# Last group of a PEER layer: gate and residual folded in earlier, last v tiles loaded earlier, final norm in a written order

## The chip, the cores and the metric

The kernel runs on one core of a Trainium2 chip. The metric is the device time of one execution in microseconds (us); 3119.42 is the median of three runs. Engines: PE multiplies matrices into PSUM banks, DVE, ACT and POOL work on SBUF and PSUM tiles, SP issues the loads and stores, POOL also issues the indexed loads (gathers). Each engine works through its own list in order and stops at a step whose data or buffer isn't there yet.

## The reference

```python
# 1024 tokens, width 1024; first sub-layer (projection, convolution + RWKV-7 scan, norm) gives x
h2 = adaln(x, shift2, scale2)
# 8 heads pick 16 of 16384 experts each: experts, gates
u_sel = jnp.take(peer_u, eb, axis=0)
z = jnp.einsum('td,tkd->tk', hb, u_sel)
act = jax.nn.gelu(z, approximate=False) * gb
y2 = jnp.einsum('tk,tkd->td', act, jnp.take(peer_v, eb, axis=0))
x = layer_norm(ALPHA * x + gate2 * y2, ln2_g, ln2_b)
```

## The kernel before

The first 1300 us (the front part) compute the first sub-layer, the routing and `x1`, the input of the last residual. Then the expert layer runs in two ways side by side.

Five of the eight token tiles of 128 rows (NT = 5, `DT` gives their numbers) are computed densely: 32 groups of four blocks of 128 experts. In a group, each block e has an up part (192 products for all four, in eight PSUM banks `mg` one after another, three banks in all), then ACT applies gelu (L1420), DVE multiplies with the routing weights `gmat` (L1422), ACT and DVE split the result into `ah` and `al` (L1423, L1424). Then comes the down part, `down(t, half, p)`: for each tile and half of the width 12 products of `ah`, `al` with the group's v tiles, and DVE adds the bank to `y_acc` (L1452). The weights come on SP as `uraw` and `vraw` through three common buffers; ACT and POOL split them (`split_w`, L1314, L1316). A group reads four v tiles, c = 0 to 3; c = 0, 1 serve the first half of the width, 2, 3 the second.

The other three tiles (`GT`) are gathered: `gather(t)` fetches one u row or v row per token and selected expert, 256 gathers of 512 KB a tile, issued by POOL (L1273) into `grow` buffers (GBUF = 7, and one `gland` buffer once space is free), each used up by one DVE step (L1279 for u, L1286 for v, summed in `gy`, a PSUM tile). `gather_to` advances these by the share of the groups that is done, so that all are called for by group 30; `residual_norm` ends a tile. A scheduler, which knows what each step needs, sets the order of the steps on each engine; the code sets priorities.

In group 31 the v tiles are multiplied by the gate on DVE (`vraw`, L1312) before they are split, so that the last products come out gated. `finish` loads v tiles 2 and 3, loads `x1` of the five tiles into `xres`, gates `y_acc` (L1358, three tiles on DVE, two on POOL), adds ALPHA times `x1` (L1363 on DVE, L1360 and L1361 on ACT and POOL), then adds each bank (L1372, with the row sum; L1375 and bn_stats for the last tile), gets the variance from squares on ACT (L1383), scales on ACT (L1391), multiplies with the norm's gain (L1392) and adds its offset (L1393) on DVE and stores the halves (L1394).

Of the kernel before, what the change touches and what calls it, by code (L numbers as in the profile page):

```python
# [60 lines left out]
FT = 5  # L61
FV = 3
# [33 lines left out]
def layer_kernel(ctx, tc, x, cols, c_row, cond_w, w_in, w2a2, g2, w_out, ln_rows, wq, keys, peer_u, peer_ut, peer_v, peer_vt, out):  # L96
# [136 lines left out]
    def rsqrt(mv):  # L233

        rs = small.tile([128, 1], F32, name="rstd")
        nr = small.tile([128, 1], F32, name="rnew")
# [2 lines left out]
        V.tensor_mul(nr, rs, rs)
# [1000 lines left out]
    more, turn = [], [0]  # L1240

    def landing():
# [5 lines left out]
        if more and turn[0] % (GBUF + 1) == 0:  # L1248
# [3 lines left out]
    def gather(t):  # L1252
# [17 lines left out]
        for i in range(256):  # L1270
            while k < 256 and len(pend) < GBUF - 1 + len(more):
# [74 lines left out]

    def finish(down, vs):
        vs += [load_v(31, 2), load_v(31, 3)]
        xts = []
        for t in range(NT):  # L1350
            xts.append(de.tile([128, D], F32, tag="raw" if t < 2 else "uhi" if t < 4 else "ulo", name="xres",
                               bufs=3 if t < 2 else 2))
            ld(xts[t], x1_d[DT[t]])
        row_pair([(1, ln_rows[3])])
        gather_to(1)
        for t in range(NT):
            E = V if t < FV else G
            E.tensor_mul(y_acc[:, t], y_acc[:, t], lnr[2])  # L1358
            if t >= FV:
                A.activation(xts[t], xts[t], AF.Copy, scale=ALPHA)  # L1360
                G.tensor_add(xts[t], xts[t], y_acc[:, t])  # L1361
            else:
                V.scalar_tensor_tensor(xts[t], xts[t], ALPHA, y_acc[:, t], op0=OP.mult, op1=OP.add)  # L1363
        for t in range(NT):
            xt = xts[t]
            st = small.tile([128, 2, 6], F32, name="bnst")
            sums = small.tile([128, 4], F32, name="fsum")
            for half, hs in enumerate(halves):
                p = md() if half else mg()
                down(t, half, p)  # L1370
                if t < NT - 1:
                    V.scalar_tensor_tensor(xt[:, hs], p, 1.0, xt[:, hs], op0=OP.mult, op1=OP.add,  # L1372
                                           accum_out=sums[:, half:half + 1])
                else:
                    V.tensor_add(xt[:, hs], p, xt[:, hs])  # L1375
                    V.bn_stats(st[:, half, :], xt[:, hs])
            b = small.tile([128, 1], F32, name="nbias")
            if t < NT - 1:
                mv = small.tile([128, 2], F32, name="bnmv")
                V.tensor_scalar(mv[:, 0:1], sums[:, 0:1], sums[:, 1:2], -1.0 / D, op0=OP.add, op1=OP.mult)  # L1380
                sq = grow()
                for half, hs in enumerate(halves):
                    A.activation(sq[:, hs], xt[:, hs], AF.Square, bias=mv[:, 0:1], accum_out=sums[:, 2 + half:3 + half])  # L1383
                V.tensor_scalar(mv[:, 1:2], sums[:, 2:3], sums[:, 3:4], 1.0 / D, op0=OP.add, op1=OP.mult)
                m, r = rsqrt(mv)
                V.tensor_mul(b, m, r)
            else:
                m, r = moments(st)
                V.scalar_tensor_tensor(b, m, -1.0, r, op0=OP.mult, op1=OP.mult)
            for hs in halves:  # L1390
                A.activation(xt[:, hs], xt[:, hs], AF.Identity, bias=b, scale=r)  # L1391
                V.tensor_mul(xt[:, hs], xt[:, hs], lnr[0][:, hs])  # L1392
                (V if t >= NT - 1 - FT else G).tensor_add(xt[:, hs], xt[:, hs], lnr[1][:, hs])  # L1393
                ld(out[128 * DT[t]:128 * DT[t] + 128, hs], xt[:, hs])  # L1394
# [3 lines left out]
    for g in range(32):  # L1398
        gm = g_next
        if g < 31:  # L1400
            g_next = load_g(g + 1)
# [109 lines left out]
```

## Time and profile before

| what | value |
|---|---|
| timed runs | 3113.9, 3119.42, 3121.65 us |
| profiled execution | 3138.46 us, of which the span is 3136.6 |
| busy: PE, DVE, POOL, ACT | 2958.2, 2386.3, 1808.7, 1187.2 us |
| last product on PE | starts at 3116.09 us |
| last store, on SP | issued at 3133.2 us |

Times in the rows are us from the start of the span: a row of the engines in order of time has start, duration, engine, line, operation, output and inputs with shapes, and in brackets how long the engine stood before it and what ended that. Line numbers (L1286) are those of the kernel before. For the kernel after, lines move: the gathers' steps are L1300 and L1307, the gmat step L1530, `al` L1532, the sums L1560, the gate on v L1333, `fold` L1355 to L1357, and all steps written through `InOrder` carry L1382.

### The profile page before, as it was taken

The page shows a single profiled execution, that of the slowest core. Times are in us where ns is not written, and L with a number is a line of the kernel's source. Part 1 is how long each engine was busy: PE and PEld are TensorE (multiplying, and loading weights), DVE is VectorE, ACT ScalarE, POOL GpSimd, SP SyncE. Part 2 cuts the span into 40 slices and gives each one's busy share as a digit, 9 for nine tenths or more (in the row PEclk, how much of TensorE's full clock was granted, in tenths as well). Part 3 has the DMA queues.
Part 4 walks back from the last instruction along what each step waited for, and adds up shares of the span by engine and source line. Part 5 has one row for each costly group of instructions (what it writes and reads, how often), then busy time and mean ns, then how long its engine had stood idle before and what let it go on. Part 6 is the DMA issues. An engine that isn't in the chain of part 4 may idle for free.

```text
span 3136.6 us, 54848 instructions
## 1 busy us (share of the span) xinstructions
PE 2958.2 (94%) x20416; PEld 2616.1 (83%) x20416; DVE 2386.3 (76%) x5392; ACT 1187.2 (38%) x2238; POOL 1808.7 (58%) x1419
## 2 busy tenths in 40 slices
PE   6979998989899789999999999999999999999997
PEld 4748667878778688898898899989999898999986
DVE  6276654446876989369999999997778787777878
ACT  5562443333345657842332233322223132222324
POOL 2434112223352443477777786877778688787774
PEclk9989998968888999999999999999999999999999
DMA  8878857768666797899999999999999999999995
GB/s 318 307 206 310 263 153 217 259 217 298 216 220 241 281 330 287 330 339 346 321 331 336 313 338 322 346 356 340 337 336 339 335 337 348 331 340 347 329 353 190
DMA packets 431851, 945.77 MB, mean 302 GB/s; under 512 B 92464, under 2 KB 234208, under 8 KB 411104
## 3 DMA queue, kind: packets, MB, share of 16 engines
q1 hardware_dynamic: 318112, 497.62, 47.0%
q0 software_dynamic: 110592, 402.70, 34.4%
q10 hardware_dynamic: 2880, 41.94, 3.3%
q8 instruction: 160, 2.62, 0.3%
q14 instruction: 107, 0.88, 0.1%
HBM read 800.76 MB, written 141.39 MB: 300 GB/s over the span
## 4 chain that ended last, share of the span: by engine, by line
PE 61%; DVE 18%; DMA 5%; ACT 3%; issue 3%; POOL 1%; SPq 1%; DVEq 0%; ACTq 0%; POOLq 0%
PE mg L1418 23%; PE md L1434 21%; PE mm L216 5%; PE mm L870 2%; DVE grow L1279 2%; PE mgate L1108 1%; PE mm L528 1%; DMA cw<-cond_w 1%; DVE gy L1286 1%; DVE mask L1094 1%; DVE yacc L1452 1%; PE bank L733 1%; PE bank L707 1%; PE bank L675 1%; ACT oa L1100 1%
## 5 line engine op out<-in xcount | busy, mean ns | idle before, releaser
L1418 PE MATMUL mg<-h2h,uhi 128*128 128x320 f32 x2024 | 626.8, 310 | 8.2 <-DVE al L1424 8.2
L1418 PE MATMUL mg<-h2h,ulo 128*128 128x320 f32 x2024 | 626.0, 309 | 0.1
L1418 PE MATMUL mg<-h2l,uhi 128*128 128x320 f32 x2024 | 625.5, 309 | 0.0
L1434 PE MATMUL md<-vhi,al 128*128 128x512 f32 x1260 | 490.6, 390 | 0.0
L1434 PE MATMUL md<-vlo,ah 128*128 128x512 f32 x1260 | 489.1, 390 | 0.0
L1434 PE MATMUL md<-vhi,ah 128*128 128x512 f32 x1260 | 484.9, 390 | 0.2 <-issue 0.2
L1286 DVE SCALAR_TENSOR_TENSOR gy<-grow,gz,gy 128x1024 f32<-128x1024 f32 x349 | 446.2, 1279 | 6.5 <-DMA grow<-peer_v,eid 5.5
L1279 DVE SCALAR_TENSOR_TENSOR grow<-grow,gh 128x1024 f32<-128x1024 f32 x363 | 435.5, 1209 | 16.0 <-DMA grow<-peer_u,eid 15.8
L1273 POOL DMA_INDIRECT grow<-peer_u,eid x363 | 342.6, 944 | 171.1 <-DVE grow L1279 57.3
L1273 POOL DMA_INDIRECT grow<-peer_v,eid x352 | 332.9, 946 | 164.8 <-DVE gy L1286 69.5
L1418 PEld LDWEIGHTS mg<-h2h,uhi 128*128 128x128 f32 x2024 | 380.5, 188 | 16.2 <-DVE al L1424 11.0
L1418 PEld LDWEIGHTS mg<-h2l,uhi 128*128 128x128 f32 x2024 | 380.5, 188 | 5.9
L1418 PEld LDWEIGHTS mg<-h2h,ulo 128*128 128x128 f32 x2024 | 380.4, 188 | 3.8 <-POOL ulo L1316 0.6
L1316 POOL TENSOR_TENSOR vlo<-vraw,vhi 128x1024 fp32r<-128x1024 f32 x128 | 309.1, 2416 | 35.3 <-ACT vhi L1314 31.8
L1316 POOL TENSOR_TENSOR ulo<-uraw,uhi 128x1024 fp32r<-128x1024 f32 x128 | 309.3, 2416 | 19.3 <-ACT uhi L1314 17.0
L1452 DVE TENSOR_TENSOR yacc<-md,yacc 128x512 f32<-128x512 f32 x300 | 204.8, 685 | 136.0 <-PE md L1434 94.7
L1434 PEld LDWEIGHTS md<-vlo,ah 128*128 128x128 f32 x1260 | 236.5, 188 | 47.4
L1101 POOL TENSOR_TENSOR ob<-mask,selt 128x384 f32<-128x384 bf16 x160 | 140.2, 890 | 234.2 <-DVE mask L1094 99.4
L1434 PEld LDWEIGHTS md<-vhi,ah 128*128 128x128 f32 x1260 | 236.1, 188 | 45.1 <-issue 0.6
L1434 PEld LDWEIGHTS md<-vhi,al 128*128 128x128 f32 x1260 | 236.5, 188 | 44.1
L1314 ACT ACTIVATE vhi<-vraw 128x1024 fp32r<-128x1024 f32 x128 | 134.9, 1054 | 335.8 <-DMA vraw<-peer_vt 311.2
L216 PE MATMUL mm<-hhi,wsplit 128*128 128x512 f32 x672 | 228.0, 413 | 8.5 <-ACT gsig L399 5.4
(430 smaller groups left out, 5778.9 us busy)
## 6 DMA issues: line engine op xcount, KB each, us to landing
uraw<-peer_ut SPq DMA_DIRECT2D x128, 512.0 KB
vraw<-peer_vt SPq DMA_DIRECT2D x128, 512.0 KB
wsplit<-split_wq SPq DMA_DIRECT2D x48, 1024.0 KB
G_d<-stage ACTq DMA_DIRECT2D x20, 2048.0 KB
gmat<-G_d SPq DMA_DIRECT2D x32, 1024.0 KB
cw<-cond_w SPq DMA_DIRECT2D x48, 512.0 KB
wsplit<-split_w_out SPq DMA_DIRECT2D x24, 1024.0 KB
split_w_in<-wsplit SPq DMA_DIRECT2D x22, 1024.0 KB
```

The costliest lines, as they stand in the source:

```text
L216: T.matmul(pt, l[:, k, :], r[k], start=i == 0, stop=i == 3 * KD - 1)
L528: T.matmul(pt[:, 128 * g:128 * g + 128], dg[:, 128 * j:128 * j + 128], ubuf[ct][:, g, LAGS - 1 - m:LAGS - 1 - m + 128], start=m == 0, stop ...
L870: T.matmul(acc[t], l[k][:, ts], r, start=k == 0 and q == 0, stop=k == KD - 1 and q == 2)
L1101: G.tensor_mul(ob[:, :3], mb[:, :3], gt[:, c:c + 3, None].to_broadcast([128, 3, 128]))
L1273: G.indirect_dma_start(out=r, out_offset=None, in_=peer_u if k < 128 else peer_v, in_offset=bass.IndirectOffsetOnAxis(ap=eid[:, k % 128:k ...
L1279: V.scalar_tensor_tensor(r, r, 1.0, ht, op0=OP.mult, op1=OP.mult, accum_out=z[:, i:i + 1])
L1286: V.scalar_tensor_tensor(y, r, z[:, i - 128:i - 127], y, op0=OP.mult, op1=OP.add)
L1314: A.activation(hi, raw, AF.Copy)
L1316: G.tensor_sub(lo, raw, hi.bitcast(F32))
L1418: T.matmul(p, l[:, k, :], r[k][:, bs], start=i == 0, stop=i == 3 * KD - 1)
L1434: T.matmul(p, l[:, ts], r[:, e % 2, :], start=e == 0 and q == 0, stop=e == 3 and q == 2)
L1452: ins = V.tensor_add(ya, p, ya)
```

## The change

1. `fold(t)` is called in the second half of group 29's down part, for each tile behind its last sum of that group: it loads `x1` of the tile into the one `gland` buffer, multiplies `y_acc` of the tile by the gate row and adds ALPHA times `x1`, both on DVE. Groups 30 and 31 now both get gated v tiles (before, 31 alone). The gate row is loaded in group 28 into a buffer of its own. The `gland` buffer is given up by the gathers for the last 70 (XLAST).
2. In group 31 all four v tiles are loaded with the four u blocks.
3. Gathers are called for by group 29 in place of 30, but the last 8 steps (HELD), seven gathers and the third tile's norm, are left to `finish`, which places them between the sums.
4. `finish` is written as one order for DVE, ACT and POOL (`InOrder` chains each step behind the one before on its engine; the gathered tile's norm is not chained). Tiles 0 to 2: ACT scales, POOL multiplies with the gain and adds the offset. Tile 3: DVE subtracts the mean and multiplies with the gain (read from PSUM), ACT scales, POOL adds. Tile 4: DVE does both.
5. `residual_norm` takes row sums from the residual step and squares from ACT in place of bn_stats; `rsqrt` has two fused steps in place of three.

```diff
-FT = 5
-FV = 3
+FOLD = 30
+XLAST = 70
+HELD = 8
...
-        V.tensor_mul(nr, rs, rs)
         V.tensor_scalar(mv[:, 1:2], mv[:, 1:2], LN_EPS, -0.5, op0=OP.add, op1=OP.mult)
-        V.tensor_scalar(nr, nr, mv[:, 1:2], 1.5, op0=OP.mult, op1=OP.add)
-        V.tensor_mul(rs, rs, nr)
+        V.scalar_tensor_tensor(nr, rs, mv[:, 1:2], rs, op0=OP.mult, op1=OP.mult)
+        V.scalar_tensor_tensor(rs, nr, 1.5, rs, op0=OP.add, op1=OP.mult)
...
+    def squares(xt, sums):
+        mv = sums[:, 4:6]
+        V.tensor_scalar(mv[:, 0:1], sums[:, 0:1], sums[:, 1:2], -1.0 / D, op0=OP.add, op1=OP.mult)
+        sq = grow()
+        for i, hs in enumerate(halves):
+            A.activation(sq[:, hs], xt[:, hs], AF.Square, bias=mv[:, 0:1], accum_out=sums[:, 2 + i:3 + i])
+        V.tensor_scalar(mv[:, 1:2], sums[:, 2:3], sums[:, 3:4], 1.0 / D, op0=OP.add, op1=OP.mult)
+        return mv
...
     def residual_norm(t, acc):
...
-        parts = [xt[:, 0:512], xt[:, 512:1024]]
-        normalize(parts, parts)
+        mv = squares(xt, sums)
         r = bcast_row(ln_rows[2])
-        V.tensor_mul(xt, xt, r)
+        V.scalar_tensor_tensor(xt, xt, mv[:, 0:1], r, op0=OP.add, op1=OP.mult)
+        m, rs = rsqrt(mv)
         r = bcast_row(ln_rows[3])
+        A.activation(xt, xt, AF.Copy, scale=rs)
         G.tensor_add(xt, xt, r)
...
+    def spare():
+        return bool(more) and done[0] < n_side - XLAST
...
-        if more and turn[0] % (GBUF + 1) == 0:
+        if spare() and turn[0] % (GBUF + 1) == 0:
             return more[0].tile([128, D], F32, name="gland")
...
-        while side and done[0] < frac * n_side:
+        while side and done[0] < min(frac * n_side, n_side - HELD):
...
-        if g == 31 and c % 2 == 0:
+        gated = g >= FOLD
+        if gated and c % 2 == 0:
...
+    def fold(t):
+        xt = more[0].tile([128, D], F32, name="gland")
+        ld(xt, x1_d[DT[t]])
+        V.tensor_mul(y_acc[:, t], y_acc[:, t], lnr[2])
+        V.scalar_tensor_tensor(y_acc[:, t], xt, ALPHA, y_acc[:, t], op0=OP.mult, op1=OP.add)
...
+        def add(t, half):
...
+            down(t, half, p)
+            if t < end:
+                v.scalar_tensor_tensor(yt, p, 1.0, yt, op0=OP.mult, op1=OP.add, accum_out=sums[t][:, half:half + 1])
             else:
+                v.tensor_add(yt, p, yt)
+                v.bn_stats(st[t][:, half, :], yt)
...
+        def root(t):
+            n = small.tile([128, 1], F32, name="rnew")
+            v.reciprocal(rs[t], rs[t])
+            v.tensor_scalar(mv[t][:, 1:2], mv[t][:, 1:2], LN_EPS, -0.5, op0=OP.add, op1=OP.mult)
+            v.scalar_tensor_tensor(n, rs[t], mv[t][:, 1:2], rs[t], op0=OP.mult, op1=OP.mult)
+            v.scalar_tensor_tensor(rs[t], n, 1.5, rs[t], op0=OP.add, op1=OP.mult)
+
+        def scale(t):
+            b = small.tile([128, 1], F32, name="nbias")
+            v.tensor_mul(b, mv[t][:, 0:1], rs[t])
+            for hs in halves:
+                yt = y_acc[:, t, hs]
+                a.activation(yt, yt, AF.Identity, bias=b, scale=rs[t])
+                gq.tensor_mul(yt, yt, lnr[0][:, hs])
+                gq.tensor_add(yt, yt, lnr[1][:, hs])
+                ld(out[128 * DT[t]:128 * DT[t] + 128, hs], yt)
+
+        def centre(t):
+            for hs in halves:
+                v.scalar_tensor_tensor(zt[t][:, hs], y_acc[:, t, hs], mv[t][:, 0:1], gain[0][:, hs],
+                                       op0=OP.subtract if t == end else OP.add, op1=OP.mult)
+
+        def offset(t):
+            for hs in halves:
+                z = zt[t][:, hs]
+                if t == end:
+                    v.scalar_tensor_tensor(z, z, rs[t], lnr[1][:, hs], op0=OP.mult, op1=OP.add)
                 else:
+                    a.activation(z, z, AF.Copy, scale=rs[t])
+                    gq.tensor_add(z, z, lnr[1][:, hs])
+                ld(out[128 * DT[t]:128 * DT[t] + 128, hs], z)
+
+        add(0, 0); gathers(2); add(0, 1); mean(0); gathers(2); add(1, 0); var(0); gathers(2)
+        add(1, 1); root(0); scale(0); mean(1); gathers(1); add(2, 0); var(1); gathers(1)
+        add(2, 1); root(1); scale(1); mean(2); gathers(1)
+        gain[0] = psy.tile([128, D], F32, tag="ghy", name="gain")
+        a.activation(gain[0], lnr[0], AF.Copy)
+        add(3, 0); var(2); add(3, 1); root(2); scale(2); mean(3); add(4, 0); centre(3); var(3)
+        add(4, 1); mean(4); root(3); offset(3); centre(4); root(4); offset(4)
...
-            row_pair([(2, mod_d[5].rearrange("a b -> (a b)")), (0, ln_rows[2])])
+            row_pair([(0, ln_rows[2]), (1, ln_rows[3])])
...
-            if e > 1:
-                vs.append(load_v(g, e - 2))
+            if e > 1 or g == 31:
+                vs.append(load_v(g, e if g == 31 else e - 2))
...
-            gather_to((g + e / 8) / 30)
+            gather_to((g + e / 8) / 29)
...
+                if g == FOLD - 1 and half:
+                    fold(t)
```

(The calls of `finish` stand one to a line in the code.) What the scheduler makes of it at three places, each engine's own list:

DVE in the up part of group 30, before. `gy` steps use up a gather, `mg` and `al` steps belong to the up products:

```order
L1422 TENSOR_TENSOR mg_30359<-mg_30359,gmat_29723 128x320
L1286 SCALAR_TENSOR_TENSOR gy_27826<-grow_29555,gz_25265,gy_27826 128x1024
L1424 TENSOR_TENSOR al_30329<-mg_30359,ah_30328 128x320
L1286 SCALAR_TENSOR_TENSOR gy_27826<-grow_29578,gz_25265,gy_27826 128x1024
L1422 TENSOR_TENSOR mg_30402<-mg_30402,gmat_29723 128x320
L1286 SCALAR_TENSOR_TENSOR gy_27826<-grow_29595,gz_25265,gy_27826 128x1024
```

DVE at that place after the change, from the fold of the third tile to that of the fourth (`gland` holds `x1`):

```order
L1357 SCALAR_TENSOR_TENSOR yacc_14208<-gland_30162,yacc_14208 128x1024
L1307 SCALAR_TENSOR_TENSOR gy_27436<-grow_29079,gz_24947,gy_27436 128x1024
L1530 TENSOR_TENSOR mg_30309<-mg_30309,gmat_29750 128x320
L1333 TENSOR_TENSOR vraw_30419<-vraw_30419,md_30344 128x1024
L1307 SCALAR_TENSOR_TENSOR gy_27436<-grow_29082,gz_24947,gy_27436 128x1024
L1530 TENSOR_TENSOR mg_30355<-mg_30355,gmat_29750 128x320
L1532 TENSOR_TENSOR al_30279<-mg_30309,ah_30278 128x320
L1307 SCALAR_TENSOR_TENSOR gy_27436<-grow_29085,gz_24947,gy_27436 128x1024
L1532 TENSOR_TENSOR al_30354<-mg_30355,ah_30353 128x320
L1307 SCALAR_TENSOR_TENSOR gy_27436<-grow_29108,gz_24947,gy_27436 128x1024
L1357 SCALAR_TENSOR_TENSOR yacc_14208<-gland_30180,yacc_14208 128x1024
```

The residual steps and the gate on v have moved in between the up part's steps, where there were gathers and up steps alone.

SP over the same group, before (the last digits of `x_d_` and `G_d_` number the tensor):

```order
L1310 DMA uraw<-peer_ut 128x1024 x2
L1310 DMA vraw<-peer_vt 128x1024
L1310 DMA uraw<-peer_ut 128x1024
L1310 DMA vraw<-peer_vt 128x1024 x3
L1310 DMA uraw<-peer_ut 128x1024
```

SP there after the change (`x_d_106` to `x_d_109` are `x1` of the second to the fifth tile):

```order
L1331 DMA uraw<-peer_ut 128x1024 x2
L1331 DMA vraw<-peer_vt 128x1024
L1355 DMA gland<-x_d_106 128x1024
L1331 DMA uraw<-peer_ut 128x1024
L1355 DMA gland<-x_d_107 128x1024
L1331 DMA vraw<-peer_vt 128x1024
L1355 DMA gland<-x_d_108 128x1024
L1331 DMA vraw<-peer_vt 128x1024 x2
L1355 DMA gland<-x_d_109 128x1024
L1331 DMA uraw<-peer_ut 128x1024
```

The loads of `x1` now stand between the weights' loads; before, they came in group 31, with one weight tile left behind the first of them.

ACT at the end, before, from the scaling of the gathered tile on (`grow` is the gathered tile in the first row, a scratch tile in the others):

```order
L250 ACTIVATE grow<-grow,nbias,rstd 128x512 x2
L1383 ACTIVATE grow,fsum<-xres,bnmv 128x512 x6
L237 ACTIVATE rstd<-bnmv,eps_ln 128x1 x3
L1383 ACTIVATE grow,fsum<-xres,bnmv 128x512 x2
L1391 ACTIVATE xres<-xres,nbias,rstd 128x512 x6
```

ACT at the end after the change, from the gathered tile's squares on (`rstd` steps are square roots, `gain` the copy to PSUM):

```order
L1233 ACTIVATE grow,bnst<-grow,bnst 128x512 x2
L238 ACTIVATE rstd<-bnst,eps_ln 128x1
L1253 ACTIVATE grow<-grow,rstd 128x1024
L1382 ACTIVATE yacc<-yacc,nbias,rstd 128x512 x2
L1382 ACTIVATE grow,bnst<-yacc,bnst 128x512 x2
L1382 ACTIVATE gain<-gmat 128x1024
L1382 ACTIVATE rstd<-bnst,eps_ln 128x1
```

Squares of one tile and scalings of the tile before it now alternate, with the gathered tile's steps and the copy of the gain among them; before, all squares came first.

More of the change, by code (lines that the diff above doesn't have):

```diff
@@ L1270, in gather @@
         for i in range(256):
[L1271 removed]
+            while k < 256 and len(pend) < GBUF - 1 + spare():
                 r = landing()
@@ L1345, in load_g @@
         return t
[L1347 to L1361, printed above, removed]
-            else:
[L1363 to L1373, printed above, removed]
-                else:
[L1375 to L1394, printed above, removed]
@@ new lines, in layer_kernel, with __init__, __getattr__, issue @@
+    class InOrder:
+        def __init__(self, engine):
+            self.engine, self.last = engine, None
+        def __getattr__(self, name):
+            def issue(*a, **k):
+                with tc.issue_after(self.last.ins) if self.last else nullcontext():
+                    self.last = getattr(self.engine, name)(*a, **k)
+                return self.last
+            return issue
+    def finish(down):
+        v, a, gq = InOrder(V), InOrder(A), InOrder(G)
+        sq = grow()
+        end = NT - 1
+        st, sums, mv, rs = {}, {}, {}, {}
+        zt = {t: de.tile([128, D], F32, tag="raw", name="zres", bufs=3) for t in (end - 1, end)}
+        gain = {}
+        def gathers(n):
+            with tc.issue_after(v.last.ins):
+                for _ in range(n):
+                    step(side)
+        def add(t, half):
+            hs, yt = halves[half], y_acc[:, t, halves[half]]
+            if half == 0:
+                st[t] = small.tile([128, 2, 6], F32, name="bnst")
+                sums[t] = st[t].rearrange("p a b -> p (a b)")
+                mv[t] = sums[t][:, 4:6] if t < end else small.tile([128, 2], F32, name="bnmv")
+            p = md() if half else mg()
+            down(t, half, p)
+            if t < end:
+                v.scalar_tensor_tensor(yt, p, 1.0, yt, op0=OP.mult, op1=OP.add, accum_out=sums[t][:, half:half + 1])
+            else:
+                v.tensor_add(yt, p, yt)
+                v.bn_stats(st[t][:, half, :], yt)
+        def mean(t):
+            rs[t] = small.tile([128, 1], F32, name="rstd")
+            if t == end:
+                v.bn_aggr(mv[t], st[t])
+                a.activation(rs[t], mv[t][:, 1:2], AF.Sqrt, bias=eps_ln)
+                return
+            v.tensor_scalar(mv[t][:, 0:1], sums[t][:, 0:1], sums[t][:, 1:2], -1.0 / D, op0=OP.add, op1=OP.mult)
+            for i, hs in enumerate(halves):
+                a.activation(sq[:, hs], y_acc[:, t, hs], AF.Square, bias=mv[t][:, 0:1],
+                             accum_out=sums[t][:, 2 + i:3 + i])
+        def var(t):
+            v.tensor_scalar(mv[t][:, 1:2], sums[t][:, 2:3], sums[t][:, 3:4], 1.0 / D, op0=OP.add, op1=OP.mult)
+            a.activation(rs[t], mv[t][:, 1:2], AF.Sqrt, bias=eps_ln)
+        def root(t):
[20 more added lines that the diff above has]
+                z = zt[t][:, hs]
+                if t == end:
+                    v.scalar_tensor_tensor(z, z, rs[t], lnr[1][:, hs], op0=OP.mult, op1=OP.add)
+                else:
+                    a.activation(z, z, AF.Copy, scale=rs[t])
+                    gq.tensor_add(z, z, lnr[1][:, hs])
+                ld(out[128 * DT[t]:128 * DT[t] + 128, hs], z)
+        add(0, 0)
+        gathers(2)
+        add(0, 1)
+        mean(0)
+        gathers(2)
+        add(1, 0)
+        var(0)
+        gathers(2)
+        add(1, 1)
+        root(0)
+        scale(0)
+        mean(1)
+        gathers(1)
+        add(2, 0)
+        var(1)
+        gathers(1)
+        add(2, 1)
+        root(1)
+        scale(1)
+        mean(2)
+        gathers(1)
+        gain[0] = psy.tile([128, D], F32, tag="ghy", name="gain")
+        a.activation(gain[0], lnr[0], AF.Copy)
+        add(3, 0)
+        var(2)
+        add(3, 1)
+        root(2)
+        scale(2)
+        mean(3)
+        add(4, 0)
+        centre(3)
+        var(3)
+        add(4, 1)
+        mean(4)
+        root(3)
+        offset(3)
+        centre(4)
+        root(4)
+        offset(4)
+        assert not side
```

23 lines of the change are left out of this document (14 added, 9 removed).

## The prediction

> **What bounds the kernel now.** I read the span and clock first, then the busy time by stretches, the engines' instructions in order of time over the last 140 us, and the chain that ended last.
>
> ```profile
> core 0: 3136.6 us, clock 0.963
> 0.00:300.00 300.00, 245.01 (x1313) 188.38 (x1314) 169.60 (x346) 139.16 (x241) 110.67 (x79) 0.93 0.83 286
> 2900.00:3090.00 190.00, 190.00 (x1095) 175.33 (x1094) 156.06 (x183) 54.37 (x91) 150.78 (x111) 1.00 0.91 328
> 3090.00:3137.00 47.00, 25.80 (x113) 20.68 (x111) 39.06 (x99) 20.59 (x39) 10.61 (x4) 0.83 0.33 129
> 2951.38 25.96 PE mg L1418 x177
> 3006.65 26.10 PE mg L1418 x178
> ```
>
> The stretches give PE, PEld, DVE, ACT and POOL busy, then granted clock, DMA share and GB/s. From 2900 to 3090 PE is busy all the time, DVE 82%, POOL 79%, DMA 91%: the dense groups are PE's, one every 55.3 us (the two chain rows that open the up products of groups 29 and 30), with every helper near full. After 3090 PE is done half-way and DVE is busy for 39 of 47 us. So the end of the kernel is DVE's, and there the change acts.
>
> ```profile
> 3110.88 0.39 PE L1434 MATMUL md<-vhi,ah 128*128 128x512 f32 x1
> 3116.09 0.39 PE L1434 MATMUL md<-vlo,ah 128*128 128x512 f32 x1
> 3120.89 0.69 DVE L1392 TENSOR_TENSOR xres<-xres,gmat 128x512 f32<-128x512 f32 x1
> 3121.49 0.68 DVE L1393 TENSOR_TENSOR xres<-xres,gmat 128x512 f32<-128x512 f32 x1
> 3131.94 1.28 DVE L1393 TENSOR_TENSOR xres<-xres,gmat 128x512 f32<-128x512 f32 x2
> ```
>
> The last product ends at 3116.48 (call it E), DVE's last multiply-add pair at 3133.2, the span at 3136.6: 20.1 us behind E, of which the last 3.4 us are the last store. Between the two PE rows lie 23 steps, 0.2265 us a product; a 128x512 DVE step is 0.60 us (the two rows after them).
>
> **The tail, after the change.** When tile 0's last products begin, 107 of group 31's 120 down products are still to come (the order puts 13 earlier): they begin at A = E - 24.3. The order now lets DVE do, from A on, eight sums with accumulation, seven gathers, the third gathered tile's norm, two plain sums, two bn_stats, four half-tile multiplications in `centre`, two in `offset` and about 37 one-column steps. The durations:
>
> ```profile
> 3063.49 1.28 DVE L1286 SCALAR_TENSOR_TENSOR gy<-grow,gz,gy 128x1024 f32<-128x1024 f32 x1
> 3064.68 0.49 DVE L1422 TENSOR_TENSOR mg<-mg,gmat 128x320 f32<-128x320 f32 x1
> 3065.08 1.28 DVE L1286 SCALAR_TENSOR_TENSOR gy<-grow,gz,gy 128x1024 f32<-128x1024 f32 x1
> 3074.86 1.21 DVE L1312 TENSOR_TENSOR vraw<-vraw,md 128x1024 f32<-128x1024 f32 x1
> 3075.99 0.49 DVE L1422 TENSOR_TENSOR mg<-mg,gmat 128x320 f32<-128x320 f32 x1
> 3105.17 0.69 DVE L1372 SCALAR_TENSOR_TENSOR xres<-mg,xres 128x512 f32<-128x512 f32 x1
> 3105.78 0.08 DVE L1372 DVE_READ_ACCUMULATOR xres<-mg,xres 128x1 f32 x1
> 3105.78 0.69 DVE L1372 SCALAR_TENSOR_TENSOR xres<-mg,xres 128x512 f32<-128x512 f32 x1
> 3116.55 0.29 DVE L239 TENSOR_TENSOR rnew<-rstd 128x1 f32<-128x1 f32 x3
> 3111.66 0.71 ACT L1383 ACTIVATE grow<-xres,bnmv 128x512 f32<-128x512 f32 x1
> 3112.37 0.71 ACT L1383 ACTIVATE grow<-xres,bnmv 128x512 f32<-128x512 f32 x1
> 3118.14 4.32 ACT L1391 ACTIVATE xres<-xres,nbias,rstd 128x512 f32<-128x512 f32 x6
> 3099.63 1.04 ACT L1360 ACTIVATE xres<-xres 128x1024 f32<-128x1024 f32 x1
> ```
>
> From start to start a gather takes 1.19 us, another full-width step 1.13, a sum with its accumulator 0.69 (its read comes at 0.61 and the next sum may start with it; I take both), a one-column step about 0.08. ACT takes 1.45 for two squares or two scalings of a tile and 1.04 for a full-width copy. DVE's own work is then 8x0.69 + 7x1.19 + 1.13 (gate row) + 1.38 + 1.13 (the gathered tile) + 10x0.60 + 37x0.08 = 26.5 us, against 41 us from A to the last DVE end before. Left out are the residual sums and the late v tile, and ten multiply-add pairs, of which POOL takes three tiles.
>
> But the order is fixed, and DVE waits in it for ACT. Step by step, us after A: first sum at 2.9; four sums, four gathers, tile 0's mean and variance to 10.6; tile 0's root and two more gathers to 13.4; the last gather and tile 2's first sum to 15.4. ACT scales tile 0 and squares tile 1 to 16.3, so tile 1's variance waits 1.0. Gate row, second sum, residual: 19.9. The gathered tile's squares hold DVE 1.5, its square root 0.3; its multiplication ends at 23.4, tile 3's first sum at 24.4. ACT has meanwhile copied the gathered tile (1.04), scaled tile 1 and squared tile 2, to 27.4: tile 2's variance waits 3.0. The gain copy (1.04) stands before tile 2's square root on ACT, another 0.6. Then tile 2's root 29.3, tile 4's first half 30.5, `centre(3)` 31.7, 0.4 for ACT's squares, second half and its sums 33.6, root 33.9, `centre(4)` 35.1, root 35.5, `offset(4)` 36.7, store 3.4: 40.1, or E + 15.8. That is 4.3 us sooner than before. PE's six banks are free in time (each is two tiles old), so PE still ends at E.
>
> One cost is not in that sum.
>
> ```profile
> 3098.19 2.41 POOL L1316 TENSOR_TENSOR vlo<-vraw,vhi 128x1024 fp32r<-128x1024 f32 x1 [1.22 <-ACT vhi L1314]
> 3100.75 3.16 POOL L1361 TENSOR_TENSOR xres<-xres,yacc 128x1024 f32<-128x1024 f32 x1 [0.15 <-ACT xres L1360]
> 3098.38 3.30 DVE L1363 SCALAR_TENSOR_TENSOR xres<-xres,yacc 128x1024 f32<-128x1024 f32 x1
> 3102.40 1.52 DVE L239 TENSOR_TENSOR rnew<-rstd 128x1 f32<-128x1 f32 x1
> 3051.39 1.22 DVE L1358 TENSOR_TENSOR yacc<-yacc,gmat 128x1024 f32<-128x1024 f32 x1
> 3050.33 0.94 POOL L1273 DMA_INDIRECT grow<-peer_v,eid  x1 [0.30 <-issue]
> ```
>
> The last two rows belong to the next part. In the first four a DVE step with two SBUF operands stands until POOL's step is over (3.30 instead of 1.2; 1.52 instead of 0.1), then POOL's until DVE's. Now POOL works on tiles 0 to 2 and on tile 3's addition through that stretch, 1.2 us a half (half of 2.41). Nine DVE steps there have two SBUF operands: three in root and bias of tile 2, two in each of the next roots, two in `offset(4)`. The wait is between 0 and 9x1.2 = 10.8 us. I take 3: POOL often has nothing scaled yet, and where it has, half of its step is over. Tail: -4.3 + 3 = -1.3 us, from -4.3 to +6.5.
>
> **The fold, in groups 29 and 30.** Ten full-width DVE steps (gate multiplications and residual) and four gated v tiles come in, 14x1.13 = 15.8 us; six of the same width go from the end of group 30 and from group 31. The up part of group 30 then holds on DVE 16x0.40 (0.40: gmat step to gather, above) + 12x1.19 + 8x1.13 = 29.7 us, against 28.1 us of PE (55.3 less 120 down products of 0.2265; eight blocks of 3.5). What covers the rest: three banks, by which PE may run a block (3.5 us) ahead of DVE, and 36 up products of group 31 that PE now has amid group 30's down products, 5.3 us. What eats it: each x1 load goes into the one `gland` buffer, so it is issued only when the step before has read it, with 6 to 9 us of DVE work until it is needed.
>
> ```profile
> 2977.07 0.33 SPq L1310 DMA_DIRECT2D uraw<-peer_ut  x1
> 2983.80 1.06 ACT L1314 ACTIVATE uhi<-uraw 128x1024 fp32r<-128x1024 f32 x1 [2.32 <-DMA uraw<-peer_ut]
> 2993.95 0.33 SPq L1310 DMA_DIRECT2D vraw<-peer_vt  x1
> 3005.25 1.06 ACT L1314 ACTIVATE vhi<-vraw 128x1024 fp32r<-128x1024 f32 x1 [20.38 <-DMA vraw<-peer_vt]
> ```
>
> A load of that size was waited for 6.7 and 11.3 us after its issue. So three loads are late by 0 to 4 us each, and a u or v tile that stands behind an x1 load on SP is late with it; PE then waits 0 to 5 us at the end of group 30's up part. I take 2, nearer the 6.7. [...]
>
> The same steps also touch the gathers: a DVE multiplication beside a gather's issue on POOL.
>
> ```profile
> 3051.58 1.85 POOL L1273 DMA_INDIRECT grow<-peer_v,eid  x1 [0.30 <-DVE yacc L1452]
> 3055.87 1.67 POOL L1273 DMA_INDIRECT gland<-peer_v,eid  x1 [0.85 <-DVE gy L1286]
> ```
>
> Both ran beside an L1358 multiplication and took 0.7 to 0.9 more than the usual 0.94. Ten such steps cost POOL up to 9 us, and POOL is full to 79%, so 0.21x110 = 23 us are free in two groups: hidden, unless the gathers fall behind, which is in the 0 to 5. [...]
>
> **What costs nothing.** The pace of gathers, 29 for 30: both orders hold 25 or so a group, paced by POOL and the buffers. One landing buffer less for the last 70: six buffers at 55.3/25 = 2.2 us are 13 us; the two waited-for gathers below came 11.5 and 12.7 us after their issue.
>
> ```profile
> 3076.30 0.94 POOL L1273 DMA_INDIRECT grow<-peer_v,eid  x1 [0.31 <-DVE vraw L1312]
> 3077.55 0.93 POOL L1273 DMA_INDIRECT gland<-peer_v,eid  x1 [0.30 <-issue]
> 3087.79 1.29 DVE L1286 SCALAR_TENSOR_TENSOR gy<-grow,gz,gy 128x1024 f32<-128x1024 f32 x1 [0.49 <-DMA grow<-peer_v,eid]
> 3090.35 1.29 DVE L1286 SCALAR_TENSOR_TENSOR gy<-gland,gz,gy 128x1024 f32<-128x1024 f32 x1 [1.27 <-DMA gland<-peer_v,eid]
> ```
>
> `rsqrt` with one step less saves 0.1 us a call on a DVE that is 57% busy in the first 300 us. It also lets the planner order the front part anew: 55 us of PE idle in those 300, which could move by some us either way; I take 0.
>
> **Sum.** -1.3 + 2 = +0.7 us on a span of 3136.6 (3138.46 with what lies around it). The three timed runs have a median of 3119.42, 19 us below the profiled one; the same difference there gives 3120.1, say 3120.
>
> **Rivals.** Faster: the DVE chain runs at its own work, ACT is never late and POOL never in the way: 2.9 + 26.5 + 3.4 = 32.8 after A, 11.6 sooner, 3108. For it speaks that ACT is 44% busy in the last 47 us; against it that tile 1's and 2's squares stand behind other tiles' scalings in ACT's order. Slower: the fold's loads. If each takes 11.3 us, the three come 2, 3 and 5 late, and two v tiles behind them on SP 5 each. With the 1.6 that DVE is over PE that is 21.6; the cover of 8.8 is gone, PE waits 12.8, and 3119.4 - 1.3 + 12.8 is 3131. It decides from 20 us of lateness, where PE's wait passes 10.7. Slower as well: POOL in the way of all nine steps, +6.5 and the 2: 3128. No gain because the end merely changes hands, from pairs on DVE to waits on ACT, is the forecast itself.
>
> **How the numbers follow.** No change (within 0.3%, 9.4 us, about what a measurement of this kernel can tell from none) 0.58; the fast chain 0.24, which most of faster rests on; the loads 0.1, POOL in the way 0.08. The range reaches to 3106, the fast chain with 2 us from the front part, and to 3132, both slow cases in part: about one in ten outside at either end.
>
> **What would show it.** Right: the last product ends within 5 us of 3116 and the span 14 to 20 us later; waits of tile 2's variance for ACT's squares near 3 us; `rnew` or `offset` steps on DVE drawn out to 1 us and more beside POOL. Wrong: under 12 us between the last product and the end; PE idle over 5 us in group 30; DVE waiting for `gland` in several places; or a front part that is 5 us longer or shorter.

## The result, and the profile after

The changed kernel takes 3163.95 us (median of 6 runs, 3160.2 to 3168.1) against 3122.32 for the one before in the same runs (6, 3113.9 to 3125.6): ratio 1.0126, 95% interval 1.0108 to 1.0145, some 40 us slower. The forecast was 3120. Its profiled execution took 3161.81 us. The kernel before was profiled a second time, since its first profile, 3138.46 us, lay above all of its first six timed runs.

Span and clock of the changed kernel, and its busy time by stretches (PE, PEld, DVE, ACT, POOL, then granted clock, DMA share, GB/s):

```profile
core 0: 3160.0 us, clock 0.959
0.00:300.00 300.00, 244.02 (x1297) 187.30 (x1298) 167.21 (x332) 139.41 (x241) 111.01 (x79) 0.93 0.82 282
2900.00:3110.00 210.00, 207.04 (x1166) 190.00 (x1165) 176.35 (x201) 57.89 (x97) 157.19 (x116) 0.98 0.88 314
3110.00:3160.00 50.00, 23.98 (x106) 19.52 (x104) 33.64 (x79) 18.69 (x39) 21.47 (x17) 0.79 0.41 145
```

A piece of its chain that ended last, behind PE's wait, and its last product:

```profile
3030.83 6.41 PE mg L1526 x24
```

```profile
3133.60 0.39 PE L1542 MATMUL md<-vlo,ah 128*128 128x512 f32 x1
```

PE now idles 3 us between 2900 and 3110, where before it was busy without a gap from 2900 to 3090; 24 up products behind that take 6.41 us in place of 3.5; the last product ends at 3133.99, the span 26.0 later, not 20.1. And all of it stands later already when group 0 begins. Cut at three points (group 0's first gmat step, group 29's, the last product), the profiled executions read, in us:

| profile | to group 0 | group 0 to 29 | group 29 to last product | last product to end | span |
|---|---|---|---|---|---|
| before, first | 1336.7 | 1616.5 | 163.3 | 20.1 | 3136.6 |
| before, second (b_again) | 1323.9 | 1617.8 | 162.3 | 19.3 | 3123.3 |
| after | 1343.4 | 1622.2 | 168.4 | 26.0 | 3160.0 |
| b_rsqrt | 1352.2 | 1622.4 | 162.7 | 19.2 | 3156.5 |
| b_pad | 1333.0 | 1612.3 | 163.4 | 20.6 | 3129.2 |
| b_pad2 | 1333.9 | 1618.2 | 162.3 | 20.1 | 3134.5 |
| b_ts | 1340.2 | 1614.8 | 162.3 | 20.6 | 3137.8 |
| a_oldrsqrt | 1328.1 | 1620.2 | 167.2 | 26.2 | 3141.7 |
| o_fold31 | 1335.3 | 1622.5 | 169.6 | 27.6 | 3154.9 |
| o_nopool | 1330.4 | 1622.0 | 167.3 | 20.1 | 3139.8 |
| o_lnr | 1314.8 | 1623.8 | 167.3 | 23.1 | 3129.0 |
| o_nofold | 1334.6 | 1621.9 | 162.5 | 24.1 | 3143.1 |
| o_held0 | 1326.1 | 1622.0 | 171.7 | 23.5 | 3143.3 |
| o_spread_ts | 1329.0 | 1620.0 | 162.6 | 21.5 | 3133.2 |
| o_best | 1326.5 | 1615.1 | 162.6 | 21.8 | 3126.0 |
| a_best | 1343.5 | 1621.1 | 162.6 | 21.7 | 3149.0 |

From before's second profile to after it is 19.5 + 4.4 + 6.1 + 6.7 = 36.7 us. The last two columns hardly scatter from run to run; the first does, by 22 us even with one and the same order of the front (1314.8 to 1336.7 in the ten profiles of before, a_oldrsqrt and the o_ kernels). So changes at the end are read from one profile, and the front from timed runs.

The front by stretches, up to group 0, from 400 to 520 and from 460 to 500, in the second profile of before and then in that of after:

```profile
0.00:1324.00 1324.00, 1176.71 (x10492) 995.73 (x10493) 865.82 (x2695) 664.76 (x1371) 458.08 (x391) 0.93 0.76 264
400.00:520.00 120.00, 114.96 (x1237) 85.81 (x1237) 67.61 (x126) 51.01 (x94) 16.05 (x13) 0.99 0.59 169
460.00:500.00 40.00, 36.83 (x348) 27.53 (x349) 23.14 (x45) 19.77 (x33) 4.70 (x5) 0.96 0.70 195
```

```profile
0.00:1343.00 1343.00, 1186.75 (x10488) 998.71 (x10489) 862.92 (x2670) 660.99 (x1367) 459.49 (x391) 0.92 0.75 260
400.00:520.00 120.00, 114.45 (x1084) 82.27 (x1081) 63.68 (x119) 47.33 (x86) 13.62 (x11) 0.90 0.59 168
460.00:500.00 40.00, 35.14 (x316) 26.22 (x314) 28.57 (x50) 18.07 (x33) 7.50 (x6) 0.70 0.59 149
```

PE's waits there (us in total, times, longest), before and after, and the product that closes the second half's input projection, before and after (duration in ns, start):

```profile
PE mgate L1108 <- ACT oa L1100: 11.1, 22, 1.6
```

```profile
PE mgate L1108 <- ACT oa L1100: 22.1, 22, 7.0
PE bank L753 <- DVE Q L750: 12.7, 2, 12.2
```

```profile
L493 PE MATMUL mm<-ident,mod x1: 272/272/272, 512.5 to 512.5; 128*48 128x128 f32 x1
```

```profile
L493 PE MATMUL mm<-ident,mod x1: 270/270/270, 526.9 to 526.9; 128*48 128x128 f32 x1
```

The number of products is the same within four. PE stands 156 us in place of 147, and is busy 10 us longer; the granted clock is lower, 0.90 in place of 0.99 from 400 to 520, around which that projection ends 14 us later. Two waits stand out, 11 us more on ACT's `oa` and 12.7 on DVE's `Q` of the scan; others are shorter, so that 9 us remain.

This is no accident of one pair of profiles. The ten profiles with before's front order and the three with after's (after, b_rsqrt, a_best) differ in each of these numbers without overlap:

| up to group 0 | ten, before's order | three, after's order |
|---|---|---|
| granted clock, 460 to 500 | 0.91 to 0.96 | 0.70 |
| last product of that projection starts | 507.5 to 521.6, mean 513.4 | 526.3 to 528.9, mean 527.4 |
| PE's waits for `Q` on DVE, to 1320 | none in the lists of waits | 12.7 |
| PE's waits for `oa` on ACT, to 1320 | 8.9 to 13.4 | 18.9 to 20.3 |
| group 0 begins | 1314.8 to 1336.7, mean 1328.5 | 1343.4 to 1352.2, mean 1346.4 |

So 14 of the 18 us are there by 527. The 12.2 us wait for `Q` and the waits for `oa` come behind 760, after most of the lateness. The lower clock from 460 to 500 alone is worth by estimate 40 x (0.925 - 0.70) = 9 us of full-clock work (0.925 is the mean of the ten).

### The profile page after: what moved, and what is told of

Read it like the earlier page. It is cut to its first block, busy times and chain, and to the rows that moved or that the text cites. A ratio compares the mean times of both kernels' runs of the same rounds, so it can differ in the third digit from the quotient of the medians.

```text
span 3160.0 us, 54823 instructions
## 1 busy us (share of the span) xinstructions
PE 2965.5 (94%) x20416; PEld 2618.1 (83%) x20416; DVE 2380.5 (75%) x5352; ACT 1187.3 (38%) x2243; POOL 1822.5 (58%) x1429
## 4 chain that ended last, share of the span: by engine, by line
PE 46%; DVE 7%; issue 2%; DMA 2%; POOL 1%; ACT 1%; DVEq 0%; SPq 0%; ACTq 0%; POOLq 0%
PE mg L1526 24%; PE md L1542 22%; DVE grow L1300 1%; DVE gy L1307 1%; DVE yacc L1560 1%; DMA grow<-peer_u,eid 1%; DMA vraw<-peer_vt 1%; POOL grow L1294 0%; DVE ltkg L1031 0%; DVE mg L1530 0%; ACT oa L1100 0%; DVE loh L1023 0%; DMA grow<-peer_v,eid 0%; POOL ulo L1337 0%; DVE al L1532 0%
## 5 line engine op out<-in xcount | busy, mean ns | idle before, releaser
L1307 DVE SCALAR_TENSOR_TENSOR gy<-grow,gz,gy 128x1024 f32<-128x1024 f32 x357 | 456.9, 1280 | 4.5 <-DMA grow<-peer_v,eid 3.2
L1294 POOL DMA_INDIRECT grow<-peer_v,eid x360 | 344.2, 956 | 172.9 <-DVE gy L1307 71.5
L1526 PEld LDWEIGHTS mg<-h2h,uhi 128*128 128x128 f32 x2024 | 382.8, 189 | 20.6 <-DVE al L1532 15.0
L1337 POOL TENSOR_TENSOR ulo<-uraw,uhi 128x1024 fp32r<-128x1024 f32 x128 | 309.4, 2417 | 30.2 <-ACT uhi L1335 28.1
```

The source lines that it names most:

```text
L1294: G.indirect_dma_start(out=r, out_offset=None, in_=peer_u if k < 128 else peer_v, in_offset=bass.IndirectOffsetOnAxis(ap=eid[:, k % 128:k ...
L1307: V.scalar_tensor_tensor(y, r, z[:, i - 128:i - 127], y, op0=OP.mult, op1=OP.add)
L1337: G.tensor_sub(lo, raw, hi.bitcast(F32))
L1526: T.matmul(p, l[:, k, :], r[k][:, bs], start=i == 0, stop=i == 3 * KD - 1)
```

## The experiments

Names: b_ kernels are the one before with one edit; a_oldrsqrt is the changed kernel with before's square root; o_ kernels are a_oldrsqrt with a further edit. The order of a_oldrsqrt is before's, and that of b_rsqrt is after's, on every engine up to the first late tile's norm, so the two split the change cleanly. (In the traces up to 1300 us, 11 of DVE's 2672 steps in a_oldrsqrt fall out of before's order, 12 of 2675 between the two profiles of before, and some 1350 in after.)

**b_again**: no edit.

> The kernel before, unchanged, for a second profile. The first one took 3138.5 us, some 16 us more than the timed executions (3122.3). Theory A (the front part: the shorter square-root chain gave it another order, and that costs most of the 41.6 us): a profile of an ordinary execution has its lead over the first one ahead of the dense groups, the first gmat step of group 0 at 1317 to 1325 us instead of 1336.7. Theory B (the end: fold, held gathers, pinned tail): the lead is spread over the dense groups and the first gmat step stays within 5 us of 1336.7.

3125.25 us. First gmat step at 1323.9; everything behind it took 1799.4 us in place of 1799.9. So the first profile's extra 13 us lay in the front, as theory A said.

**b_rsqrt**

```diff
-        V.tensor_mul(nr, rs, rs)
         V.tensor_scalar(mv[:, 1:2], mv[:, 1:2], LN_EPS, -0.5, op0=OP.add, op1=OP.mult)
-        V.tensor_scalar(nr, nr, mv[:, 1:2], 1.5, op0=OP.mult, op1=OP.add)
-        V.tensor_mul(rs, rs, nr)
+        V.scalar_tensor_tensor(nr, rs, mv[:, 1:2], rs, op0=OP.mult, op1=OP.mult)
+        V.scalar_tensor_tensor(rs, nr, 1.5, rs, op0=OP.add, op1=OP.mult)
```

> The kernel before with the changed kernel's square root alone (one DVE step less a call), which gives it the changed kernel's front order up to the first late tile's norm. Theory A: 20 to 32 us slower than before, 3143 to 3155. Theory B: within 7 us of before's 3122. A mixture is possible; what this run does not show of the 41.6 us has to come from the fold, the gathers or the end.

3151.48 us (4 runs), ratio 1.0065 (1.0039 to 1.0092): 20 us (12 to 29, at the lower edge of theory A), with group 0 at 1352.2, 24 later than the mean of before's order, and the end as before. Saving a step of 0.1 us costs about half of the loss.

**a_oldrsqrt**: the same diff reversed, on the changed kernel.

> The changed kernel with the square root of before (one DVE step more a call), which gives it before's front order. Theory A: 8 to 16 us slower than before (fold about 6 and end about 5 by the two profiles), 3130 to 3139. Theory B: 30 to 42 us slower, 3152 to 3164, as the changed kernel.

3143.40 us (5 runs), ratio 1.0047 (1.0032 to 1.0062): 15 us (10 to 19). That is theory A's 8 to 16 by the difference; by the absolute time it lies 4 us above A's range, since before took 3128.16 in the same runs. The loss has two parts, and 20 + 15 = 35, within the interval of the whole (34 to 45).

**b_pad, b_pad2**: b_rsqrt with one copy, and with two, of a 128x1 value in the chain; each gives the front another order.

```diff
         V.scalar_tensor_tensor(nr, rs, mv[:, 1:2], rs, op0=OP.mult, op1=OP.mult)
+        V.tensor_copy(nr, nr)
         V.scalar_tensor_tensor(rs, nr, 1.5, rs, op0=OP.add, op1=OP.mult)
```

> The kernel before with the two-step square root and one further DVE copy of a 128x1 value between them, so that a call has as many DVE steps as before, while the planner's order of the front part is a third one (DVE differs from its 31st instruction on). Theory A1 (what costs is the order that the planner happened to give; the steps themselves weigh nothing): the time may fall on either side, anywhere from 3110 to 3150, and the trace shows the difference to before as already there at the first gmat step of group 0, with the dense part behind it within 5 us. Theory A2 (the fused steps are themselves slower than those they replace, or the shorter chain is what the planner handles badly): as b_rsqrt, 3143 to 3155, whatever the order; or with the longer chain as before, within 5 us of it.

3131.37 us (10 runs), ratio 1.0008 (0.9996 to 1.0019).

> The kernel before with the two-step square root and two further 128x1 DVE copies in the chain, one step more than before: a fourth order of the front part. Theory A1 (an order drawn anew, good or bad without regard to the chain's length): the first gmat step of group 0 anywhere from 1310 to 1355 us, and the time different from before's by the same amount within 8 us. Theory A2 (a shorter chain is what harms): as before or faster, first gmat step at 1315 to 1337 as in the six profiles with before's front order.

3140.81 us (10 runs), ratio 1.0052 (1.0035 to 1.0069); its profiled run, 3136.2, was the fastest of the ten. The fused steps are in all three kernels; with one copy they cost nothing that can be told, with none 20 us, with two, a longer chain than before's, 16. So the fused steps don't explain the loss, and it needs no short chain. Group 0 began at 1333.9 in that profile, 5 us later than the mean of before's order, so that 11 of the 16 us aren't seen there, more than the 8 that theory A1 allowed; a profile of the fastest run can't settle it.

**b_ts**: as short a chain as b_rsqrt's, in another instruction.

```diff
+        V.tensor_scalar(nr, rs, mv[:, 1:2], rs, op0=OP.mult, op1=OP.mult)
+        V.tensor_scalar(rs, nr, 1.5, rs, op0=OP.add, op1=OP.mult)
```

> The kernel before with the square root in as few DVE steps as the changed kernel, but with tensor_scalar and 128x1 scalars in place of scalar_tensor_tensor: by that the planner orders the front part a fifth way. Theory A1 (the order drawn decides): time from 3110 to 3155, and unlike b_rsqrt's (20 us over before) by more than 8. Theory A2' (a chain that is one step shorter is what harms, in whatever order): 3140 to 3155, as b_rsqrt.

3139.01 us (10 runs), ratio 1.0050 (1.0032 to 1.0068). By the medians 11 us from b_rsqrt, by the ratios 5 (16 against 20), and the intervals overlap: this run doesn't tell the two apart. With b_pad2, the order as such remains the reading that fits; it is inferred, not shown by this run. That a short chain harms besides isn't excluded: both kernels that have one are slow. All four redrawn orders lie at before's time or on the slow side of it.

**o_nofold**: `fold` returns at once, so y gets neither gate multiplication nor residual.

> The changed kernel with before's square root and the fold's steps on y left out (no gate multiplication, no x1 loads, no residual; the output lacks them), the v tiles of groups 30 and 31 gated as before. Theory B1 (the fold's DVE steps make PE wait and then run at a lower clock): no PE wait behind group 29, and from group 29's first gmat step to the last product 162 to 164 us instead of 167.2, as in the kernel before (162.3 and 163.3). Rival B3 (the gathers' pace or the gated v tiles are what delays PE): 165 to 168.

162.5 us from group 29 to the last product and no PE wait: B1. The fold is the whole of that loss (its DVE steps and its loads of `x1`, which this run doesn't part); neither the gathers' pace nor the gated v tiles cost anything there.

**o_fold31**: FOLD 31 in place of 30.

> The changed kernel with before's square root (3143 timed, first gmat step to end 1813.4 us in its profile, 13.8 more than before's) and the fold behind group 30 instead of group 29. Theory B1 (the fold's DVE steps beside group 30's up part make PE wait, and the short wait costs clock as well): the stretch from group 29's first gmat step to group 31's last loses 4 to 6 of the 6 to 7 us that it is longer than before, 1807 to 1810 in all. Rival B2 (the fold merely has no room in two groups of which DVE is the fuller engine, so the wait moves along with it into group 31): the same 13 to 16 us, shifted.

169.6: B2. The wait moves to the next group and grows (5.0 us, at one place). From group 0 to the end this profile took 1819.7, 20 over before's, more than B2's 13 to 16.

**o_lnr**: the last gathered tile's norm takes the rows that `finish` has.

```diff
-        r = bcast_row(ln_rows[2])
+        r = lnr[0] if 0 in lnr else bcast_row(ln_rows[2])
...
-        r = bcast_row(ln_rows[3])
+        r = lnr[1] if 1 in lnr else bcast_row(ln_rows[3])
```

> As base the changed kernel with before's square root; the last gathered tile's norm takes the gain and offset rows that the end has in SBUF already, in place of two loads of its own, which stood on SP behind a store that waited for POOL. Theory D1 (the load is what DVE waited 2.3 to 2.4 us for, and the whole chain behind it): last product to end 26 to 23.5. Rival D2 (tile 2's squares on ACT take over the wait): 25 to 26.

23.1 us from the last product to the end, 3.1 less: D1.

**o_nopool**: tiles 0 to 2 without POOL's gain and offset.

> As the kernel above this one's base (changed kernel, before's square root), with POOL's gain multiplications and offset additions of tiles 0 to 2 left out, so that those three tiles are stored without gain and offset. Theory C1 (DVE's steps with two operands in SBUF stand still beside POOL): rnew and rstd steps of tiles 2 to 4 fall from 0.7 to 1.2 us to 0.15 to 0.22, 4.1 us in all, and the stretch from the last product to the end from 26 to 21 to 23. Rival C2 (the locked steps hide waits for ACT that come up instead): less than 2 us.

20.1, 6.1 less, and more than the 3 to 5 that C1 said. The wait for the rows' load is gone too (2.4 us in a_oldrsqrt), since SP's stores no longer wait for POOL (tile 0's two took 1.04 us on the queue, 2.97 in a_oldrsqrt); tile 4's two steps stay locked (0.70 and 1.19), beside tile 3's addition that POOL keeps.

**o_held0**: HELD 0.

> The changed kernel with before's square root (end 26.0 us after the last product), with no gathers held back: all of them stand ahead of the first sum of tile 0 on DVE. Theory E1 (the seven held gathers, 8.3 us of DVE work, lengthen the end): last product to end 18 to 22, last product at the same place. Rival E2 (the gathers come no sooner than landing buffers and POOL allow, about one in 2.2 us, so DVE's first sum waits for the last of them): the first sum starts 8 to 15 us later after group 31's last gmat step, PE waits for banks, and the end comes no sooner or later.

Rival E2, in part: the end is 2.7 shorter, but the last product comes 4.5 later, and group 29 to the end takes 1.8 more. DVE's and PE's waits name the cause:

```profile
DVE gy L1308 <- DMA grow<-peer_v,eid: 4.7, 3, 3.5
PE mg L1543 <- DVE yacc L1383: 2.5, 1, 2.5
```

**o_spread_ts**: o_lnr, with the fold in two halves and one-operand steps in the end's square root and `nbias`. `gate_y` has the fold's gate multiplication; `fold` keeps the load of `x1` and the residual.

```diff
                 if g == FOLD - 1 and half:
-                    fold(t)
+                    gate_y(t)
+                if g == FOLD and half:
+                    fold(t)
...
-            v.scalar_tensor_tensor(n, rs[t], mv[t][:, 1:2], rs[t], op0=OP.mult, op1=OP.mult)
+            v.tensor_scalar(n, rs[t], mv[t][:, 1:2], rs[t], op0=OP.mult, op1=OP.mult)
```

> Base: o_lnr (group 29 to last product 167.3, last product to end 22.8). Two edits at places that do not overlap. First, the fold in two halves: the gate multiplications of y stay behind group 29, the x1 loads and residual additions go to the down part of group 30. Theory B1 (too much DVE work in a row ahead of group 30's first gmat step): the PE wait of 3.0 us and the slow 24 products behind it go, 162 to 164. Rival B2 (the wait moves to group 31's up part, as with the fold behind group 30): 166 to 169. Second, the last two steps of the end's square root, and nbias, written as one-operand steps (tensor_scalar with 128x1 scalars). Theory C1 (only steps with two operands in SBUF stand still beside POOL): each takes 0.15 to 0.25 also beside POOL's steps, and 22.8 becomes 18.5 to 20. Rival C3 (any DVE step meets POOL there): 22 to 23.

162.6 us, no PE wait: B1. In the end C1 holds for the steps, in order of time on DVE:

```profile
3117.98 0.27 DVE L1386 TENSOR_SCALAR rnew<-rstd,bnst 128x1 f32<-128x1 f32 x1
3118.28 0.21 DVE L1386 TENSOR_SCALAR rstd<-rnew,rstd 128x1 f32<-128x1 f32 x1
3126.26 2.42 DVE L1386 SCALAR_TENSOR_TENSOR zres<-zres,rstd,gmat 128x512 f32<-128x512 f32 x2
```

0.27 and 0.21 beside POOL, where the two-operand forms took 0.77 and 1.18. But the end, 21.5, is only 1.6 shorter than o_lnr's, and C1's 18.5 to 20 was missed: `offset`, still with two operands, now meets POOL (2.42 for two half-tiles, 1.42 in after).

**o_best**: o_spread_ts with tile 2's moments from bn_stats on DVE. **a_best**: the same with the two-step square root in front.

```diff
+        BN = 2, end
...
-            if t < end:
+            if t not in BN:
                 v.scalar_tensor_tensor(yt, p, 1.0, yt, op0=OP.mult, op1=OP.add, accum_out=sums[t][:, half:half + 1])
```

> Before's square root in front, and all mended at the end: the last gathered tile's rows from SBUF, the fold in two halves, one-operand steps in the end's square root, and tile 2's moments by bn_stats on DVE in place of squares on ACT, whose 3.2 us of waiting then cost 1.5 of DVE work. Theory (the end's losses are found): from the last product to the end 19 to 21 (21.7 without the last edit, 20.1 and 19.2 before), from group 0's first gmat step to the end 1801 to 1804, and timed 3 to 6 us over before, within 0.3%. Rival (something else in the change costs as well): 8 to 15 over.

3130.25 us (10 runs), ratio 1.0018 (1.0000 to 1.0036): some 4 (medians) to 6 us (ratio) over before, and 9 better than a_oldrsqrt by the ratios. The last edit gave nothing: 21.8, where 19 to 21 was expected; from group 0 to the end the profile reads 1799.5, as before's 1799.4 and less than the 1801 to 1804 expected, since groups 0 to 29 were 2 us short of before's. At the end DVE is done earlier, but POOL now ends last, as the chain by line shows:

```profile
by line: POOL yacc L1386 39.7%; POOL zres L1386 13.1%; POOL grow L1255 10.6%; POOLq L1625 7.4%; DVE grow L1251 5.4%; ACT grow L1254 5.3%; issue 1.6%; DVE rnew L1386 0.8%; DVE rnew L240 0.7%; DVE rstd L1386 0.6%; DVE rnew L242 0.6%; DVE rstd
3109.13 1.24 POOL yacc L1386
3119.73 2.88 POOL zres L1386 x2
```

> As o_best, but with the changed kernel's two-step square root and so its front order. If front and end add: 20 to 28 us over before (3145 to 3153), against 39 to 42 of the changed kernel. If the front's share was part of the end's: within 10 of before.

3155.47 us (4 runs), ratio 1.0106 (1.0070 to 1.0142), 25 us over o_best in the same runs by the medians, 27 by the ratios; over before it is 29 and 33, above the range expected. So the front's share stands by itself: with the end mended, one 128x1 DVE step less per square root still costs 25 to 27 us. No version beat the kernel before; o_best lies some 34 us under the changed one (1.0018 against 1.0126 of before).

## Why the prediction was wrong

**The step that failed: "It also lets the planner order the front part anew ... I take 0".** Measured 20 us (12 to 29) by itself, 25 to 27 between a_best and o_best, and 17.8 in the profiles (mean start of group 0: 1346.4 in three with the new front order, 1328.5 in ten with before's). The prediction named a front 5 us longer or shorter as a sign of being wrong, and this sign came. It had been seen that the order moves, and 2 us were allowed for it. The size was to be had: 55 us of PE idle in 300 us were noted there, and over the front it is 147, so a new order had room of tens of us. That it would be slower and not faster could not be read from the profile of before. Why this order is slow is shown as far as this: in every profile of it the clock granted from 460 to 500 is 0.70, and 14 of the 18 us are there by 527; behind that PE waits longer for `oa` and `Q`, which other, shorter waits make up for in large part. It was not in the first 300 us, whose idle time the prediction had read: PE is busy there for 243.9 to 245.8 us in the new order, for 244.0 to 246.0 in the old one. Which swap in the order begins it, and why the clock falls there, was not tried.

**The base.** The sum was laid on a profiled execution that was 16 us slower than the median, and the same 19 us were then taken off. The slow 13 us lay in the front, which scatters; the after profile lies within 2 us of its median. Profile to profile the loss looked like 23 us, and was 42 by the medians.

**Fold, +2 (0 to 5): measured +5 to +6.** That DVE is the fuller engine there came true (its price, 29.7 against 28.1 us of PE, was not measured by itself); the cause named for the wait did not. No DVE step waited for an x1 load, so the rival of the late loads falls. DVE was simply never idle from the fold's first step to group 30's first gmat steps, and two of the ten steps met POOL's splits (1.83 and 3.21 us, the other eight 1.21 to 1.30). After, in order of time on POOL, DVE and PE:

```profile
3026.48 2.40 POOL L1337 TENSOR_TENSOR ulo<-uraw,uhi 128x1024 fp32r<-128x1024 f32 x1
3023.81 1.83 DVE L1356 TENSOR_TENSOR yacc<-yacc,gate 128x1024 f32<-128x1024 f32 x1
3026.76 3.21 DVE L1357 SCALAR_TENSOR_TENSOR yacc<-gland,yacc 128x1024 f32<-128x1024 f32 x1
3030.83 0.63 PE L1526 MATMUL mg<-h2h,uhi 128*128 128x320 f32 x1 [2.96 <-DVE al L1532]
3031.26 0.47 PE L1526 MATMUL mg<-h2l,uhi 128*128 128x320 f32 x1
3031.53 0.47 PE L1526 MATMUL mg<-h2h,ulo 128*128 128x320 f32 x1
```

The locked residual step took 3.21, PE waited 2.96, within the range. What I left out is what followed the wait on PE: the next products start 0.27 us apart, not 0.147, at a granted clock of 0.54, and 24 of them lose 2.9 us more. This term, forecast at 2, was mis-sized by 3 to 4 us.

**Tail, -1.3 (-4.3 to +6.5): measured +5.9 to +6.7.** Much of the walk came true: tile 1's variance waited 1.15 (1.0 forecast), the gathered tile's squares 1.59 (1.5), tile 2's variance 3.10 (3.0). DVE, SP and POOL of after:

```profile
3135.27 1.28 DVE L1250 SCALAR_TENSOR_TENSOR grow<-grow,bnst 128x1024 f32<-128x1024 f32 x1 [2.25 <-DMA grow<-ln_rows]
3140.64 0.21 DVE L1382 TENSOR_SCALAR bnst<-bnst 128x1 f32<-128x1 f32 x1 [3.10 <-ACT grow L1382]
3142.02 0.77 DVE L1382 SCALAR_TENSOR_TENSOR rnew<-rstd,bnst 128x1 f32<-128x1 f32 x1
3142.82 1.18 DVE L1382 SCALAR_TENSOR_TENSOR rstd<-rnew,rstd 128x1 f32<-128x1 f32 x1
3149.41 1.11 DVE L1382 SCALAR_TENSOR_TENSOR rstd<-rnew,rstd 128x1 f32<-128x1 f32 x1
3127.28 2.96 SPq L1443 DMA_DIRECT2D out<-yacc  x2
3130.49 0.91 SPq L1224 DMA_DIRECT2D grow<-ln_rows  x2
3124.57 5.30 POOL L1382 TENSOR_TENSOR yacc<-yacc,gmat 128x512 f32<-128x512 f32 x4 [12.74 <-ACT yacc L1382]
```

Of the 7.2 us between forecast (E + 18.8) and measurement (E + 26.0): 2.25 are a load that the forecast did not follow onto its queue, where it stood behind a store that waited for POOL's tile 0 (o_lnr took it away); five steps held by POOL lost 4.1 together, 1.1 over the 3 taken; tile 0's first sum ended 20.2 us ahead of E, not 21.4; the last store took 4.6 from DVE's last step, not 3.4; some 1.5 us are spread or open. The rival "POOL in the way" (+6.5) was nearest in its sum, but not by its mechanism alone.

**Right:** the gathers beside the fold. POOL's issues were stretched (1.67 to 1.76 us beside the fold's steps, 0.93 to 0.95 for the others there) and PE's one wait behind group 29 was that for DVE. (One reading there was slightly off: the second gather came 12.8 us after its issue, not 12.7, still within the 13 of six buffers.) **Open:** 2 to 6 us between groups 0 and 29, which differ by as much between runs of one order (1620.2 in a_oldrsqrt, 1623.8 in o_lnr, 1615.1 in o_best).

## What to carry to other kernels

Where a planner sets the order, an edit of one small instruction is a new draw of the whole order: build it, compare the orders, and time that edit by itself before any estimate of the rest. Keeping the number of steps does not keep the order: b_pad had as many as before. Compare profile with profile only if both lie near the median of their runs. Moving work off the end pays only if every queue it passes is followed, SP's and POOL's too, and if the engine that receives it has idle time in that very stretch.

## What the runs showed of the hardware

- In the changed kernel a PE wait of 2.96 us was followed by 24 products in 6.41 us, 0.27 each in place of 0.147, at a granted clock of 0.54; wait and slower products cost 5.9 together. In a_oldrsqrt a wait of 3.0 us was followed by 24 products in 5.21. In o_spread_ts, where PE had no wait, the granted clock stayed at 1.00 over that stretch (2997 to 3022).
- Five one-column DVE steps with two tensors in SBUF took 0.70 to 1.18 us beside POOL in the changed kernel, and those in the same places 0.21 to 0.27 with one tensor and 128x1 scalars in o_spread_ts. Not every step with two is held: the `nbias` step right behind the first two took 0.16 beside the same POOL steps.
- With one and the same order of the front, nine kernels reached group 0 at 1314.8 to 1336.7 us in ten profiles. Behind it, before's two executions differ by 0.5 us in 1799, but a_oldrsqrt, o_lnr and o_best, of one order from group 0 to 29, by up to 8.7 there.
